# Channel attention over 96 heads: TensorE's instructions rolled into a loop of sixteen heads, hand-made semaphores, single V buffers and 1 MB stores

## The chip, the cores and the metric

The kernel runs on one core of a Trainium2 chip. A core has TensorE (matrix products, PE in the profile), VectorE (DVE), ScalarE (ACT), GpSimd (POOL) and SyncE (SP), each with its own instruction stream, and 16 DMA engines that move data between HBM and the on-chip memory SBUF. TensorE writes into PSUM, a small accumulator memory. The metric is the device time of one execution in microseconds (us), the median over several runs.

## The reference

```python
batch, heads, seq, dim = 8, 12, 512, 64          # Q, K, V: float32
Q_norm = Q / (np.linalg.norm(Q, axis=-2, keepdims=True) + 1e-10)
K_norm = K / (np.linalg.norm(K, axis=-2, keepdims=True) + 1e-10)
attn = np.einsum('bhnd,bhne->bhde', Q_norm, K_norm)
attn = np.exp(attn - np.max(attn, axis=-1, keepdims=True))
attn = attn / (np.sum(attn, axis=-1, keepdims=True) + 1e-10)
return np.einsum('bhnd,bhde->bhne', V, attn).astype(np.float32)
```

For each of 96 heads a 64 x 64 attention matrix between the columns of Q and K is made (each column normed over the 512 rows), a softmax is taken along its rows, and V is multiplied by it. Q, K, V and the output are 12.58 MB each, 50.33 MB in all.

## The kernel before

**Tiling.** Four heads make a unit u (24 of them), two units a pair s (12), two pairs a window w of sixteen heads (6). A row of 128 partitions holds four heads of 32 partitions with 16 sequence rows each.

**The pieces**, named as in the plan of lines 413 to 485, each with the engine that runs it:

- lq, lk, lv (loads, SyncE; lines 178 to 200) and st (stores, SyncE; lines 202 to 210). K of pair 0 is issued from ScalarE's queue (187). One load, K of unit 3, is held back behind a small VectorE write into its buffer (185), and all loads after it too. The store of pair 9, second half, is split (204 to 208): its first half-rows go out as 92, 8 and 28 partitions.
- cq (cast of Q and K to bf16 into qkb, line 216; VectorE, ScalarE or GpSimd), mk (K masked in two copies, 222; VectorE), q2 (squares of Q, 228; ScalarE).
- gr (32 Gram matmuls a unit, 245) and nq (8 matmuls a unit for the norms of Q, 253) on TensorE, into the PSUM tile gram.
- sq, kq, hq, rd, pw, sc (lines 260 to 295): squares, a copy of the cross product, the norms' halves, their sums, the power -1/2 by Ln and Exp, and the scaling of K's side, on VectorE, ScalarE and GpSimd.
- lg (two transposes into logits, 300), ex (four exponentials with their sums, 307; ScalarE), nm (normalised blocks into ab, 316; VectorE).
- cv (cast of V into vb, 234), vt (8 transposes of V on TensorE into vps, 327), vc (their copy into vt, 333), ou (16 output matmuls, four groups a pair, 343) and oc (their copy into so, 351).

**Order.** The class Order (22 to 108) is a list scheduler that runs while the program is built: each piece has costs per engine, pieces it comes after, and a rank; of the pieces that can begin about now the one of the lowest rank is emitted. Its method pause (48) adds waiting time of TensorE for its instruction blocks. Every engine's program, TensorE's included, is then one straight list. The framework puts in the waits between engines. The helper copy (170) records most copies and casts, so in the profile lines 172, 174 and 176 are ScalarE, VectorE and GpSimd copies of many tiles.

**Buffers** (143): three of each of qk32 (2 MB), v32 (1 MB), six so (1 MB), two each of vb, vt, qkb, km, q2, four ab. In PSUM gram has two, vps one, the logits one and po two buffers; the last V transposes use a pool that takes gram's place.

## Time and profile before

| what | value |
|---|---|
| median of 3 runs (lowest to highest) | 127.64 us (127.63 to 127.68) |
| the profiled execution, span | 125.9 us |
| instructions in it | 4630 |
| HBM read and written in it | 37.75 MB and 12.58 MB, 400 GB/s over the span |
| VectorE, ScalarE, TensorE busy | 78%, 72%, 63% |

The span is that of the profiled execution from its first to its last instruction; the timed runs hold some 1.7 us around it. The page of the profile gives, in order: busy time of each engine, the span in 40 equal slices of 3.15 us with digits for tenths, the DMA queues, the chain of work that ended last, the costliest groups of instructions, and the DMA issues. A queue named "instruction" carries the engines' program text; queues of kind "hardware_dynamic" carry data.

### The profile page before, as it was taken

How to read it: one execution, taken by the hardware profiler on the slowest of the kernel's cores; microseconds unless marked ns; L12 is line 12 of the kernel's file. 1: busy time of each engine (PE TensorE's matmuls, PEld its weight loads, DVE VectorE, ACT ScalarE, POOL GpSimd, SP SyncE). 2: the span in 40 equal slices, each digit the busy share in tenths (PEclk: the TensorE clock that was granted, in tenths of full speed). 3: DMA queues.
4: the chain of work that ended last, by engine and by line, in shares of the span. 5: the costliest groups of instructions: out<-in, count | busy, mean ns of one | idle time of the engine just before them, and what ended most of it. 6: DMA issues, size and time to landing. Idle time of an engine off the chain costs nothing.

```text
span 125.9 us, 4630 instructions
## 1 busy us (share of the span) xinstructions
PE 79.6 (63%) x1944; PEld 63.9 (51%) x1944; DVE 98.8 (78%) x198; ACT 91.0 (72%) x217; POOL 50.0 (40%) x68
## 2 busy tenths in 40 slices
PE   0036949258789857766776668676794875976000
PEld 0035848236668745555665555555683764754000
DVE  3189676967959399987999989999979999999200
ACT  4243476579979999499999999999499997670000
POOL 6243353384561836633437226138743551000000
PEclk9999999955555899999999999999779999599555
DMA  3999999999999999999999999999999999999993
GB/s 105 401 419 419 422 414 418 432 424 410 439 409 418 414 433 414 410 431 419 411 428 428 403 419 423 424 424 407 426 413 420 410 415 407 417 411 404 400 411 134
DMA packets 12159, 50.63 MB, mean 402 GB/s; under 512 B 1130, under 2 KB 1130, under 8 KB 10730
## 3 DMA queue, kind: packets, MB, share of 16 engines
q1 hardware_dynamic: 11850, 49.29, 95.9%
q10 hardware_dynamic: 288, 1.05, 2.1%
q8 instruction: 15, 0.25, 0.7%
q14 instruction: 6, 0.05, 0.1%
HBM read 37.75 MB, written 12.58 MB: 400 GB/s over the span
## 4 chain that ended last, share of the span: by engine, by line
DVE 32%; ACT 24%; DMA 18%; PE 8%; issue 7%; POOL 3%; ACTq 0%; SPq 0%; POOLq 0%
DMA out_dram<-so 12%; DVE so L174 12%; DVE km L222 10%; DMA qk<-in_K_dram 6%; PE gram L245 6%; ACT vt L172 5%; ACT q L228 5%; ACT qkb L172 4%; ACT ex L307 4%; DVE ab L316 4%; DVE qkb L174 3%; ACT vb L172 2%; ACT kq L172 2%; POOL vb L176 2%; DVE n L280 1%
## 5 line engine op out<-in xcount | busy, mean ns | idle before, releaser
L245 PE MATMUL gram<-qkb,km 64*128 64x128 bf16 x768 | 33.3, 252 | 23.3 <-DVE km L222 23.3
L245 PEld LDWEIGHTS <-km 64*128 64x128 bf16 x768 | 28.3, 113 | 26.7 <-DVE km L222 26.3
L176 POOL TENSOR_SCALAR qkb<-qk 128x1024 bf16<-128x1024 f32 x24 | 25.4, 1062 | 28.6 <-PE gram L245 19.9
L222 DVE TENSOR_SCALAR km<-qkb,pick 128x1024 bf16<-128x1024 bf16 x48 | 30.3, 671 | 3.0 <-ACT qkb L172 2.4
L174 DVE COPY so<-po 128x512 f32<-128x512 f32 x48 | 30.8, 684 | 0.4
L228 ACT ACTIVATE q<-qk 128x1024 bf16<-128x1024 f32 x24 | 25.5, 1065 | 6.3 <-DMA qk<-in_Q_dram 4.3
L343 PE MATMUL po<-ab,vt 128*32 128x128 bf16 x768 | 20.1, 231 | 9.5 <-DVE so L174 6.9
L172 ACT COPY vt<-vps 128x1024 bf16<-128x1024 bf16 (+1 forms) x26 | 24.5, 956 | 1.2 <-PE vps L327 1.0
L343 PEld LDWEIGHTS <-vt 128*32 128x32 bf16 x768 | 13.4, 100 | 14.9 <-issue 10.7
L327 PE MATMUL vps<-identb,vb 128*128 128x128 bf16 x192 | 16.7, 237 | 3.0 <-ACT vt L172 2.2
L176 POOL TENSOR_SCALAR vb<-v 128x1024 bf16<-128x1024 f32 x13 | 15.0, 1156 | 8.4 <-DMA v<-in_V_dram 8.2
L307 ACT ACTIVATE ex<-lg,r 128x64 f32<-128x64 f32 x48 | 14.5, 325 | 1.6 <-PE lg L300 1.6
L327 PEld LDWEIGHTS <-vb 128*128 128x128 bf16 x192 | 12.6, 106 | 6.0 <-issue 3.1
L174 DVE CAST qkb<-qk 128x1024 bf16<-128x1024 f32 x13 | 12.1, 933 | 4.2 <-DMA qk<-in_K_dram 4.1
L293 POOL TENSOR_TENSOR kqs<-kq,r 128x256 f32<-128x256 f32 x12 | 7.9, 660 | 18.8 <-ACT r L289 8.3
L316 DVE TENSOR_TENSOR ab<-ex,rinv 64x256 bf16<-64x256 f32 x24 | 12.1, 504 | 0.6
L260 DVE SCALAR_TENSOR_TENSOR scr<-gram,eye 128x256 f32<-128x256 f32 x12 | 5.1, 424 | 8.5 <-ACT kq L172 5.7
L172 ACT CAST vb<-v 128x1024 bf16<-128x1024 f32 x11 | 11.7, 1062 | 0.0
L172 ACT CAST qkb<-qk 128x1024 bf16<-128x1024 f32 x11 | 11.6, 1054 | 0.0
L307 ACT ACTIVATION_READ_ACCUMULATOR ex<-lg,r 128x1 f32 x48 | 10.4, 217 | 0.0
L172 ACT COPY kq<-gram 128x256 f32<-128x256 f32 x12 | 4.6, 380 | 7.1 <-PE gram L253 3.1
L253 PEld LDWEIGHTS <-q 128*128 128x128 bf16 x192 | 7.5, 100 | 3.7 <-issue 2.7
(25 smaller groups left out, 41.1 us busy)
## 6 DMA issues: line engine op xcount, KB each, us to landing
out_dram<-so SPq DMA_DIRECT2D x23, 512.0 KB, 9.8
v<-in_V_dram SPq DMA_DIRECT2D x11, 1024.0 KB, 15.8
qk<-in_Q_dram SPq DMA_DIRECT2D x8, 1024.0 KB, 15.9
qk<-in_K_dram SPq DMA_DIRECT2D x8, 1024.0 KB, 17.6
qk<-in_Q_dram SPq DMA_DIRECT2D x8, 512.0 KB, 8.7
qk<-in_K_dram SPq DMA_DIRECT2D x6, 512.0 KB, 9.6
qk<-in_K_dram ACTq DMA_DIRECT2D x2, 512.0 KB
v<-in_V_dram SPq DMA_DIRECT2D x2, 512.0 KB
```

The costliest lines, as they stand in the source:

```text
L172: nc.scalar.copy(o, i)
L174: nc.vector.tensor_copy(o, i)
L176: nc.gpsimd.tensor_scalar(out=o, in0=i, scalar1=1.0, scalar2=0.0, op0=ALU.mult, op1=ALU.add)
L222: nc.vector.tensor_scalar(out=km[u][:, :, a], in0=qkb[u][:, :, 0], scalar1=pick[:, a:a + 1], scalar2=None, op0=ALU.mult)
L228: nc.scalar.activation(q2[u], qk32[s][:, 0, r], AF.Square)
L245: nc.tensor.matmul(gram[s][:, 2 * g + r, 0:2 * D], km[u][rows, t].rearrange("p a d -> p (a d)"), qkb[u][rows, t].rearrange("p x d -> p (x ...
L253: nc.tensor.matmul(gram[s][:, 0, 2 * D + HU * r:2 * D + HU * (r + 1)], q2[u][:, 2 * t:2 * t + 2].rearrange("p t d -> p (t d)"), heads, sta ...
L293: (nc.vector if eng == "DVE" else nc.gpsimd).tensor_tensor(out=kqs[s], in0=kq[s], in1=r8[s][:, 0:HU, None].to_broadcast([128, 4, D]), op=A ...
L307: nc.scalar.activation(e[:, h, :], lg[s][:, h, :], AF.Exp, scale=r8[s][:, HU + h:HU + h + 1], accum_out=z[:, h:h + 1])
L316: nc.vector.tensor_tensor(out=a[half, :, half], in0=e[half], in1=ri[half, :, None].to_broadcast([D, HU, D]), op=ALU.mult,)
L327: nc.tensor.transpose(ps[:, c, n, :], vb[w][:, J * c + j].rearrange("p r d -> p (r d)"), identb)
L343: nc.tensor.matmul(po[s, x][32 * h:32 * (h + 1), j].rearrange("p r d -> p (r d)"), v, ab[s][:, h, :])
```

## The change

The framework's tiles and waits are given up. All buffers are allocated by name, all semaphores by hand, and every piece is a generator of instructions.

- **TensorE.** Its order is written down: FRONT, five turns of one body, BACK. A turn w holds, for the pair n = 2w+2 (EVEN) and n = 2w+3 (ODD), the Gram and norm matmuls, the logits of pair n-1, transposes of V and output groups of the pairs 2w and 2w+1. The body is emitted once, in a hardware loop on TensorE alone. Inside it TensorE takes tokens: it waits until a token semaphore has reached a value and takes that value off again, so that the same instruction serves in every turn.
- **The other engines** keep straight programs, ordered by Order; pause and its parameters are gone, and all ranks and biases are new. A piece that TensorE takes inside the loop counts up a token; every other piece counts up its engine's own counter. Another engine that needs a piece counted by a token waits for a later counted piece of the same engine or for the TensorE piece that took the token.
- **Buffers.** vb and vt have one buffer instead of two, ab two instead of four, v32 four instead of three, so seven instead of six. V is cast by halves of the sequence groups that one half of vt needs.
- **Order of dependencies.** kq comes after sq, hq after kq; sq waits for the norms' matmuls too. lg waits for nm of the pair before.
- **DMA.** A pair is stored as one transfer of 1 MB, except the last, which goes in two of 512 KB. The split store and the held load are gone. SyncE waits before each transfer for the eighth last.

```diff
-    CHUNK, FETCH, FIRST = 256, 6.1, 190
-    def pause(self, begin, cost, n, done):
...
-    NB = dict(qk=3, v=3, vb=2, qkb=2, vt=2, so=6, sm=2, ab=4, km=2, q2=2)
+NQ, NV, NSO = 3, 4, 7
+EVEN = "g0 lg o0 o1 n0 va g1 n1 o2 vb o3".split()
+ODD = "g0 n0 g1 n1 o0 o1 va o2 lg o3 vb".split()
+FRONT = [("nq", 1), ("nq", 0), ("gr", 0), ("gr", 1), ("nq", 2), ("gr", 3), ("lg", 0), ("nq", 3), ("gr", 2), ("vt", 0, 0), ("vt", 0, 1)]
+BACK = [("vt", 5, 3), ("vt", 5, 2), ("ou", 10, 0), ("lg", 11), ("ou", 10, 1), ("ou", 10, 2), ("ou", 10, 3), ("ou", 11, 1), ("ou", 11, 0), ("ou", 11, 3), ("ou", 11, 2)]
...
+    for w in range(W - 1):
+        body = []
+        for half, names in enumerate((EVEN, ODD)):
+            n = 2 * w + 2 + half
+            for it in names:
+                if it[0] == "g":
+                    body.append(("gr", 2 * n + int(it[1])))
+                elif it[0] == "n":
+                    body.append(("nq", 2 * n + int(it[1])))
+                elif it == "lg":
+                    body.append(("lg", n - 1))
+                elif it[0] == "v":
+                    body.append(("vt", w + half, (2 - 2 * half) + (it == "vb")))
+                else:
+                    j = int(it[1])
+                    body.append(("ou", 2 * w + j // 2, 2 * (j % 2) + half))
+        turns.append(body)
...
-        piece(("kq", s), {"ACT": 0.35, "DVE": (0.36, BIAS["kq"])}, [("gr", 2 * s), ("gr", 2 * s + 1), back("sc", s, SM)], [], R["kq"] + 0.01 * s, cross, s)
+        piece(("kq", s), {"ACT": 0.35, "DVE": (0.36, BIAS["kq"])}, [("sq", s), back("sc", s, 2)], [], R["kq"] + G["kq"] * s)
+        piece(("hq", s), {"ACT": 0.1}, [("kq", s), back("rd", s, 2)], [], R["hq"] + G["hq"] * s)
...
-        if HELD == ("l" + "qk"[x], s, r):
-            nc.vector.memset(qk32[s][0:1, x, r, 0, 0:1], 0.0)
...
-        if (s, r) == FEW:
-            for a, b in ((0, 92), (92, 100), (100, 128)):
-                nc.sync.dma_start(out=o[a:b, :J * D], in_=i[a:b, :J * D])
-            nc.sync.dma_start(out=o[:, J * D:], in_=i[:, J * D:])
-            return
+def stored(s):
+    return (0, 1) if s >= S - STS else (None,)
+
+    def store(eng, s, r):
+        o, i = Of[s // 2, s % 2], so[s % NSO].rearrange("p r t d -> p r (t d)")
+        if r is not None:
+            o, i = o[:, r], i[:, r]
+        yield eng.dma_start(out=o, in_=i)
...
+    vb = sbuf("vb", [128, 2 * T, 2, D], BF16)
+    vt = sbuf("vt", [128, J, 128, 4], BF16)
+    ab = sbuf("ab", [128, HU, 2 * D], BF16, 2)
...
+            if k in tokens:
+                last.then_inc(token[token_of(k)], 1)
+            else:
+                last.then_inc(count[e], 1)
+                own[e] += 1
...
+    for k in lane["DMA"]:
+        if k not in early:
+            wait_for("DMA", nc.sync, list(after[k]) + sent[-Order.QUEUE:1 - Order.QUEUE], k)
+            for i in emit[k[0]](nc.sync, *k[1:]):
+                i.then_inc(dma_at[k][0], 16)
+            sent.append(k)
...
+    def tensor_piece(k, looped):
+        need = {}
+        for a in taken.get(k, ()):
+            if a in tokens:
+                need[token_of(a)] = need.get(token_of(a), 0) + 1
+            else:
+                d = engine[a]
+                need[d] = max(need.get(d, 0), value[a])
+        for n, v in need.items():
+            if n in token:
+                nc.tensor.wait_ge(token[n], v).then_inc(token[n], -v)
+            else:
+                nc.tensor.wait_ge(count[n], v)
+        for i in emit[k[0]]("PE", *k[1:]):
+            pass
+        i.then_inc(count["PE"], 1)
...
+    for k in front:
+        tensor_piece(k, False)
...
+    with nc.tensor.Fori(0, len(turns)):
+        for k in full:
+            tensor_piece(k, True)
+    for k in behind:
+        tensor_piece(k, False)
```

## The prediction

> **What bounds the kernel now.** I read the DMA rows of the page first, then its queue table, then the busy time by stage, then what SyncE's queue and TensorE wait for.

> ```profile
> PE 79.6 (63%) x1944; PEld 63.9 (51%) x1944; DVE 98.8 (78%) x198; ACT 91.0 (72%) x217; POOL 50.0 (40%) x68
> ...
> DMA  3999999999999999999999999999999999999993
> GB/s 105 401 419 419 422 414 418 432 424 410 439 409 418 414 433 414 410 431 419 411 428 428 403 419 423 424 424 407 426 413 420 410 415 407 417 411 404 400 411 134
> ...
> q1 hardware_dynamic: 11850, 49.29, 95.9%
> ...
> q8 instruction: 15, 0.25, 0.7%
> ```

> No engine is above 78%, but the 16 DMA engines are full in every slice except the first and the last. 50.33 MB of Q, K, V and output have to pass, and they pass at 400 to 439 GB/s from end to end. The queue table says what else is in that stream: 15 instruction fetches of 16 KB. They are TensorE's, since 3888 of its instructions over 15 fetches are one per 259, and 0.25 MB over 3888 is 64 bytes each. Their price: 0.7% of 16 engines over 125.9 us is 14.1 us of engine time, 0.94 us each.

> ```profile
> 12.60:112.00 99.40, 73.26 (x1764) 59.01 (x1759) 86.00 (x178) 86.09 (x213) 44.88 (x46) 0.88 1.02 419
> 112.00:119.00 7.00, 3.26 (x128) 2.06 (x127) 5.37 (x9) 0.51 (x2) 0.00 (x0) 0.85 1.02 399
> 119.00:123.00 4.00, 0.00 (x0) 0.00 (x0) 0.00 (x0) 0.00 (x0) 0.00 (x0) 0.50 0.99 404
> 123.00:126.00 3.00, 0.00 (x0) 0.00 (x0) 0.00 (x0) 0.00 (x0) 0.00 (x0) 0.50 0.29 119
> ```

> The columns are the busy time of PE, PEld, DVE, ACT and POOL, the granted clock, the DMA share and GB/s. Over the middle 99.4 us VectorE is idle 13.4 us (2.8 us in each 20.6 us that two pairs of units take, a turn of the new loop), and computing ends at 117.4 us, while the DMA engines stay full to about 123 us. So the end is set by bytes; computing is some us ahead.

> ```profile
> SPq L189 <- DVE qkb L174: 10.0, 6, 4.0
> SPq L198 <- ACT vb L172: 9.9, 3, 5.3
> ...
> SPq L210 <- DMA out_dram<-so: 8.0, 11, 1.0
> ```

> ```profile
> v<-in_V_dram SPq DMA_DIRECT2D x11, 1024.0 KB, 15.8
> ```

> ```profile
> PE gram L245 <- DVE km L222: 23.3, 18, 8.3
> PE po L343 <- DVE so L174: 6.9, 19, 1.0
> ```

> The first fence is SyncE's waits (us in total, times, longest), the second the page's DMA issues (size, median us to landing), the third TensorE's waits. SyncE does wait for buffers that computing frees, but what it issues lands 15.8 us later, of which the transfer itself is 2.5 us (1.05 MB at 419 GB/s). Some 13 us of queued transfers lie ahead of it: that is the cover of every edit to the compute side. TensorE waits most for the masked K, and for nothing that looks like a missing instruction.

> **The change, part by part.** The profiled execution's span is 125.9 us, the median of the runs 127.64, so 1.7 us lie around the span; I keep them.

> *The TensorE loop.* One turn holds 4 Gram groups of 32 matmuls, 4 norm groups of 8, 2 logit pairs, 4 V transposes of 8 and 8 output groups of 16: 324 matmuls. Five turns are 1620; the straight front has 178, the back 146, together 1944 as now, so the work is the same. The text shrinks from 3888 to 2 x (178 + 324 + 146) = 1296 instructions and some 60 waits. At 256 to a fetch these are 5 fetches instead of 15. If the body (648 instructions and about 26 token waits, 2.6 blocks) stays in the instruction memory over its turns, 10 fetches go: 10 x 0.94 / 16 = 0.59 us off the DMA stream. If it doesn't stay, nothing goes, and each of the 4 taken branches back stalls TensorE. No backward branch is in this trace, so that stall is bounded: below by 0, above by two fetches in a row, each about 1.2 us from block boundary to the packet's start (the trace's packet times against TensorE's 256th, 512th, ... instruction) and 0.94 us of packet, 4.3 us. I take 0, since before shows fetches keeping up with TensorE, and hold the other end for a rival.

> *Tokens and own semaphores.* About 26 waits a turn on TensorE's sequencer; the one such instruction before TensorE's work in this trace takes 0.05 us, 1.3 us a turn, beside 20.6 - 14 = 6 us in which TensorE is idle: 0. On the other engines, an extra semaphore instruction between two operations leaves the gap between them as small as without one (the trace's 22 cases on VectorE, median gap below zero, as the next one overlaps): 0. Operations counted by a token are seen by others only through a later operation or through TensorE, so a V buffer or a finished output row is released later by one or two operations, 1 to 2 us. Behind that wait on SyncE's queue stand all later loads and stores; the 13 us above cover it. Without that cover it would cost the delay itself, 1 to 2 us at a place.

> *Single V buffers (vb, vt), two instead of four ab, four v32, seven so.* A V copy now waits until the outputs that read the same half of vt are done. In the order EVEN, ODD the outputs of half k=0 all stand in EVEN, the transposes into that half in ODD, and the other way round, so each has half a turn (10 us) against a copy of 1 us (ACT vt, 956 ns). Cost 0 behind that; if a copy came late, the 16 matmuls of an output group (0.43 us) and their store come late with it.

> *Serial order kq after sq, hq after kq.* The chain from Gram to logits gets longer by at most 0.42 + 0.38 us (scr 424 ns, kq 380 ns). Between n1 and the logits that need them stand at least five other TensorE pieces; 0 behind these.

> *Stores of 1 MB and the fewer-partition store.* Both kernels store a pair when all four copies are done, so nothing waits longer for a larger store. Transfers issued: 72 before (23 + 11 + 8 + 8 + 8 + 6 + 2 + 2 and the 4 of L207/L208), 58 after (32 of Q and K, 13 V, 13 stores). In the trace's packet records a DMA's 16 semaphore packets take 9 ns each: 14 x 16 x 9 / 16 engines = 0.13 us. The split of L206 goes: 256 packets of 2 KB at 91 ns become 128 of 4 KB at 161 ns, (23.3 - 20.6) / 16 = 0.17 us. [...]

> *Start.* The held load (L185, SyncE's queue idle 2.7 to 7.3 us) goes; the second slice shows 401 instead of 419 GB/s, worth at most 3.15 x 18 / 419 = 0.14 us. The constants now wait for each other on GpSimd, done well before the first data at 5.5 us. I take 0 for both.

> Sum on the DMA stream: 0.59 + 0.17 + 0.13 = 0.89 us of packet time. Packet records overlap a little (share 1.02 to 1.03), so 0.85 us of span: 125.0 us, and 126.8 us as the runs count. The end is ragged now (rate falls from 122.5 to 124.7 us; about 0.9 us is lost there), and it can fall out 0.5 us either way: 126.2 to 127.4 for this case.

> **Rivals.**

> A (slower): the branch back misses. For it: the fetches of before follow TensorE block by block, one per crossing and to the very end, as of a memory that holds little more than the next block; the body is 2.6 blocks. Against it: nothing in this trace runs code twice. The price is up to 4.3 us of TensorE at each of four turns, beside 2.8 us a turn that VectorE has to spare; 1.5 us a turn stay, 6 us over four. Computing may end about 3 us later than 117.4 before the last stores (two of 1.2 us and their landing) run past 124.7, and from there it decides. With no fetch saved: 127.64 + 3 = 130.6 at the upper bound; with 2.1 us a miss, within the spare time, nothing is lost. I put it at 129.5. [...]

> B: the branch doesn't stall, or its stall is hidden, but every turn fetches its blocks anew. 13 to 15 fetches again, 0.30 us left of the gain: 127.35, at the edge of what a measurement tells.

> C (slower as well): the fixed TensorE order and the later releases starve the DMA engines in some stage. For it: SyncE waits 10.0 us for qkb and 9.9 us for vb already. Against: the queue is 13 us deep and VectorE's and ScalarE's work is the same. Half a us a turn over five turns is 2.5 us: 127.64 - 0.85 + 2.5 = 129.3.

> **How the numbers follow.** My forecast case has 0.47, A 0.19, B 0.12, C 0.22. About 0.2% (0.26 us) is what a measurement of this kernel can tell from no change, so faster means below 127.38. The forecast case lies there except for 0.04, B with half: 0.43 + 0.06 = 0.49. Same: 0.04 + 0.05 from these, and 0.02 from A with a short miss: 0.11. Slower: the rest of A and C and 0.01 of B, 0.40. The time is that of the likeliest case, 126.8. The range runs from 126.1 (all gains and a tidier end) to 130.6 (A at its upper bound); about 0.05 lies below it, 0.12 above.

> **What would show it.** TensorE's instruction queue with about 5 packets instead of 15, at the front, in the first turn and at the end: the loop stays; with 13 or more: B or A. Gaps of 2 us or more on TensorE at the start of each turn, ended by nothing the profile shows: A. DMA share of 9 in every slice from 2 to 38, near 419 GB/s: the forecast; a slice below 9 with SyncE waiting for so, vb or qkb: C. Last compute after 120 us: A or C. I am wrong if the time is above 127.4, and wrong in the reason if it is faster with 15 fetches.

## The result, and the profile after

The change makes the kernel slower.

| kernel | median (lowest to highest) | ratio to before, 95% interval | profiled span | last copy out ends | last data packet ends |
|---|---|---|---|---|---|
| before | 127.66 us (127.63 to 127.78) | 1 | 125.9 us | 117.4 us | 124.7 us |
| after | 134.59 us (133.76 to 134.85) | 1.052 [1.049, 1.055] | 133.0 us | 126.9 us | 131.2 us |

The page of the changed kernel, the rows that answer to those of before:

```profile
PE 80.8 (61%) x1944; PEld 65.8 (49%) x1944; DVE 98.0 (74%) x202; ACT 97.4 (73%) x221; POOL 36.5 (27%) x54
...
DMA  3999999999999999999999999999999999249492
GB/s 103 407 420 428 414 403 418 410 430 398 424 410 411 403 411 413 415 418 421 419 415 419 416 410 421 415 416 421 419 409 410 419 416 414 106 170 400 191 403 110
...
q1 hardware_dynamic: 11520, 49.29, 91.5%
...
q8 instruction: 5, 0.08, 0.3%
```

Five instruction fetches in place of 15, and none of them between 43.1 and 118.6 us, while the four branches back stand at 47.6, 65.0, 84.8 and 99.5: the later turns bring no fetch. But the DMA engines run dry in slices 35, 36 and 38 (113 to 126 us): all loads are done and the stores wait for results. The same stages of both kernels, after first; the columns are the busy time of PE, PEld, DVE, ACT, POOL, the granted clock, the DMA share and GB/s:

```profile
50.00:80.00 30.00, 23.55 (x608) 18.83 (x608) 27.33 (x56) 26.67 (x60) 10.99 (x11) 0.83 1.02 416
80.00:107.00 27.00, 16.39 (x390) 13.30 (x394) 22.39 (x47) 21.50 (x54) 7.13 (x8) 0.80 1.02 417
107.00:119.00 12.00, 11.16 (x294) 9.20 (x282) 11.31 (x27) 11.33 (x31) 1.97 (x4) 0.88 0.66 264
119.00:128.00 9.00, 3.90 (x130) 2.82 (x130) 7.77 (x13) 3.37 (x11) 0.37 (x1) 0.76 0.82 321
```

```profile
50.00:80.00 30.00, 21.36 (x619) 17.06 (x617) 27.57 (x57) 28.27 (x69) 13.56 (x14) 1.00 1.02 419
80.00:107.00 27.00, 18.89 (x507) 15.43 (x509) 25.19 (x52) 23.76 (x58) 12.85 (x13) 0.93 1.02 417
107.00:119.00 12.00, 8.03 (x232) 5.56 (x222) 10.18 (x20) 4.30 (x13) 0.00 (x0) 0.78 1.02 406
```

Up to 107 us the DMA share is the same 1.02, so the DMA row tells nothing of what goes wrong; the computing columns do. Before, VectorE works 25.2 of 27 us between 80 and 107 us; after, 22.4, and what is left undone stands behind 107 us. TensorE's waits in the changed kernel (us in total, times, longest):

```profile
PE gram L356 <- ACT q L336: 9.7, 1, 9.7
PE vps L410 <- PEq L658: 8.0, 3, 4.9
PE po L422 <- PEq L658: 6.8, 7, 3.1
PE gram L349 <- PEq L658: 5.4, 4, 4.0
PE vps L410 <- DVE vb L302: 5.4, 1, 5.4
```

The first row is the start, when no data is ready yet. PEq L658 is TensorE's sequencer at a token. Before, two thirds of its waiting (23.3 of 36.2 us) was for masked K; now each kind of piece in its fixed order waits for something in turn. In the timeline (start, length) one such wait and the end of VectorE's work read:

```profile
103.96 1.89 PE L349 MATMUL gram<-qkb,km 64*128 64x128 bf16 x32 [3.99 <-PEq L658]
...
125.65 1.28 DVE L302 COPY so<-po 128x512 f32<-128x512 f32 x2
```

The end of VectorE's work in the kernel before, nine copies in a row to 117.4 us:

```profile
111.88 5.48 DVE L174 COPY so<-po 128x512 f32<-128x512 f32 x9
```

The Gram group above, at a granted clock of 0.5, takes 1.89 us; a group at full clock takes 1.07 in the trace of before. How far the two have come, from the starts of the Gram groups and the ends of the copies out:

| us | Gram u4 | u8 | u12 | u16 | u20 | u23 | last copy of pair 0 | pair 6 | pair 11 |
|---|---|---|---|---|---|---|---|---|---|
| before | 20.3 | 38.8 | 54.3 | 71.2 | 88.9 | 99.7 | 50.8 | 92.8 | 117.4 |
| after | 29.2 | 48.7 | 65.8 | 85.6 | 104.0 | 113.2 | 39.2 | 95.7 | 126.9 |

Before runs its Gram matrices far ahead and does outputs late and fast; after does outputs early and Gram matrices late.

### The profile page after: what moved, and what is told of

Read it like the earlier page. It is cut to its first block, busy times and chain, and to the rows that moved or that the text cites. A ratio compares the mean times of both kernels' runs of the same rounds, so it can differ in the third digit from the quotient of the medians.

```text
span 133.0 us, 4711 instructions
## 1 busy us (share of the span) xinstructions
PE 80.8 (61%) x1944; PEld 65.8 (49%) x1944; DVE 98.0 (74%) x202; ACT 97.4 (73%) x221; POOL 36.5 (27%) x54
## 3 DMA queue, kind: packets, MB, share of 16 engines
q1 hardware_dynamic: 11520, 49.29, 91.5%
q10 hardware_dynamic: 288, 1.05, 2.1%
## 5 line engine op out<-in xcount | busy, mean ns | idle before, releaser
L349 PEld LDWEIGHTS gram<-qkb,km 64*128 64x128 bf16 x768 | 29.5, 115 | 11.6 <-issue 8.5
L300 ACT CAST qkb<-qk 128x1024 bf16<-128x1024 f32 x24 | 25.1, 1048 | 3.1 <-PE gram L349 3.1
L300 ACT COPY vt<-vps 128x1024 bf16<-128x1024 bf16 x20 | 20.3, 1016 | 5.9 <-PE vps L410 5.9
L410 PEld LDWEIGHTS vps<-identb,vb 128*128 128x128 bf16 x176 | 12.6, 113 | 17.0 <-issue 9.1
L422 PEld LDWEIGHTS po<-ab,vt 128*32 128x32 bf16 x736 | 12.7, 107 | 14.0 <-issue 11.0
L404 DVE TENSOR_TENSOR ab<-ex,ri 64x256 bf16<-64x256 f32 x24 | 14.2, 591 | 0.6
L356 PE MATMUL gram<-heads,q 128*128 128x4 bf16 x192 | 8.5, 167 | 9.7 <-ACT q L336 9.7
L302 DVE CAST vb<-v 128x1024 bf16<-128x1024 f32 x18 | 13.3, 754 | 0.2
L356 PEld LDWEIGHTS gram<-heads,q 128*128 128x128 bf16 x192 | 6.7, 99 | 12.4 <-issue 10.6
L391 PE MATMUL lg<-ident,kqs 128*128 128x128 f32 x24 | 6.9, 381 | 1.9 <-PEq L658 1.1
## 6 DMA issues: line engine op xcount, KB each, us to landing
v<-in_V_dram SPq DMA_DIRECT2D x11, 1024.0 KB, 18.6
out_dram<-so SPq DMA_DIRECT2D x11, 1024.0 KB, 12.6
qk<-in_Q_dram SPq DMA_DIRECT2D x8, 1024.0 KB, 15.3
qk<-in_K_dram SPq DMA_DIRECT2D x8, 1024.0 KB, 17.4
```

Source lines behind the costliest of these rows:

```text
L300: return nc.scalar.copy(o, i)
L302: return nc.vector.tensor_copy(o, i)
L349: yield nc.tensor.matmul(gram[s % 2][:, 2 * g + r, 0:2 * D], km[u % 2][rows, t].rearrange("p a d -> p (a d)"), qkb[u % 2][rows, t].rearran ...
L356: yield nc.tensor.matmul(gram[s % 2][:, 0, 2 * D + HU * r:2 * D + HU * (r + 1)], q2[u % 2][:, 2 * t:2 * t + 2].rearrange("p t d -> p (t d) ...
L404: yield nc.vector.tensor_tensor(out=ab[s % 2][half, :, half], in0=ex[s % 2][half], in1=ri[s % 2][half, :, None].to_broadcast([D, HU, D]), ...
L410: yield nc.tensor.transpose(v_bank(w, q)[:, c, n, :], vb[:, J * c + 2 * q + n].rearrange("p r d -> p (r d)"), identb)
```

## The experiments

Eighteen kernels, each timed beside the kernel before (127.68 to 127.86 us).

**1. Are the loop, the tokens or the buffers to blame?** First TensorE's loop is written out straight, tokens kept:

```diff
-    with nc.tensor.Fori(0, len(turns)):
-        for k in full:
+    for t in turns:
+        for k in t:
             tensor_piece(k, True)
```

> The changed kernel with its TensorE loop written out straight: five turns one after the other, same tokens, same order everywhere. Theory O (the fixed order of TensorE leaves no slack, so every late piece adds to the end): 134.6 us as the changed kernel, within 0.6, with 15 instruction fetches instead of 5. Theory L (the loop itself costs: the branch back of 0.2 us, the first pass over its blocks, the token handling at the branch): 1.5 us or more faster, 133 or below.

Measured 143.88 us (140.94 to 144.38), what neither theory said; the fastest of its runs is still 6.35 us above the changed kernel. Fifteen fetches are back. TensorE's groups in this trace (busy, mean ns, idle before and what ended it):

```profile
L349 PE MATMUL gram<-qkb,km 64*128 64x128 bf16 x768 | 36.5, 265 | 9.9 <-issue 3.9 <-PEq L658 3.3 <-DVE km L332 2.5
L422 PE MATMUL po<-ab,vt 128*32 128x128 bf16 x736 | 21.4, 252 | 10.9 <-issue 6.6 <-PEq L658 2.1 <-DVE ab L404 1.4
```

"issue", 10.5 us in these two rows, is waiting that no semaphore explains. It falls into seven gaps of 0.87 to 2.13 us, at the 1217th, 1473rd, 1985th, 2241st, 2497th, 2753rd and 3009th instruction: multiples of 256 apart, and 256 is what one fetch brings in the trace of before (16 KB at 64 bytes an instruction). I take them for blocks of text that come late. In the loop there is one such gap (1.26 us, first turn). So tokens in straight text cost more than tokens in the loop; why they bring so many late blocks was not tried. Next the tokens go too, and plain counters take their place:

```diff
-    in_loop = {k for t in turns for k in t}
+    in_loop = set()
```

> As the straight one, and no tokens: every piece counts up its engine's own counter, so that every engine sees a finished piece at once, and TensorE waits on counters. Theory O: within 0.6 us of the straight one. Theory T (pieces counted by tokens are seen late, as the store of pair 7 that is issued 6.8 us after its last copy, and buffers come free late): 2 us or more faster than the straight one.

Measured 134.58 us (133.33 to 134.94), ratio 1.052 [1.047, 1.057], last copy at 127.4 us, three late blocks (3.4 us). By its letter this is theory T's sign, but what comes back is what e1 had lost beyond the loop. Against the changed kernel nothing is gained: the loop, the tokens and the later view of their pieces do not, taken together, cost the 7 us. What each is worth alone is open, since e2 has 2.1 us more of late blocks than the loop. On this base two vb, two vt and four ab, waits loosened to match, TensorE's order kept:

```diff
-    vb = sbuf("vb", [128, 2 * T, 2, D], BF16)
-    vt = sbuf("vt", [128, J, 128, 4], BF16)
-    ab = sbuf("ab", [128, HU, 2 * D], BF16, 2)
+    vb = sbuf("vb", [128, 2 * T, 2, D], BF16, 2)
+    vt = sbuf("vt", [128, J, 128, 4], BF16, 2)
+    ab = sbuf("ab", [128, HU, 2 * D], BF16, 4)
```

> As the one without tokens, with two vb, two vt and four ab as before, and their waits relaxed accordingly; the order of every engine is kept. Theory O: within 0.7 us of the one without tokens, since the long waits of TensorE in the changed kernel are for V casts, the copy out of the single vps bank, the masked K and a po bank, none of which these buffers hold. Theory B (the single V buffers and the two ab couple the stages): 3 us or more faster.

138.72 us (138.10 to 139.16): slower still. With three v32 and six so to make room, the V transposes wait for casts of V:

```profile
PE vps L410 <- DVE vb L302: 20.8, 4, 6.6
```

The orders of the other engines were not kept, though. With the loosened waits the planner drew new ones: VectorE has 205 operations in place of 202, and its casts of V, masks and copies out follow each other differently. So this run prices neither the buffers nor the order by itself; theory B stays untested.

**2. The order.** The base of e2 takes every engine's order and assignment from the kernel before, with its buffers (two vb, two vt, four ab, three v32, six so), 512 KB stores and its dependencies of sq, kq, hq and rd:

```diff
+ORDER = [(("lq", 0, 0), "DMA"), ...]
-    front, turns, back_ = tensor_order()
+    front, turns, back_ = [k for k, e in ORDER if e == "PE"], [], []
```

> The changed kernel's machinery (buffers by name, hand-made counters, no framework waits, everything straight) running the order of before on every engine, with the buffer counts of before and stores of 512 KB. Theory O: 127.6 us as before, within 0.8, DMA full to the end, last compute near 117.4 us. Theory W (the hand-made waits, which stand as instructions of their own, cost time on the engines): 130 us or more, with last compute after 120 us.

130.43 us (130.33 to 130.52), ratio 1.021 [1.020, 1.023]; last copy at 121.5 us: what theory W had said. Whether the hand-made waits are the reason is taken up under 6. Order, assignment, these dependencies and the buffers that they need are worth 134.58 - 130.43 = 4.15 us, measured together.

**3. What does a delay cost?** TensorE is made late, in the changed order and in the kernel before:

```diff
-        for t in range(T):
+        for t in list(range(T)) * (4 if u == 10 else 1):
```

> The changed kernel written straight with counted semaphores (134.6 us by itself), and TensorE made late on purpose: the 32 matmuls of gr(10) are issued four times over, 96 matmuls more, the last pass of which leaves the same sums. One pass takes 1.1 us at the full clock and 1.9 us at half, so TensorE is held 3.3 to 5.7 us longer at that place. Theory O (the new order couples TensorE so closely to the other engines that a delay anywhere is handed on to the end): the time grows by most of the delay, 137 to 140 us. Theory L (the loss is made at a few places, above all at the end, and the DMA engines cover a delay in the middle): 134.6 within 0.7 us.

> The kernel before with the same 96 matmuls more in gr(10). Theory O says that its order has slack there, since its Gram matrices run far ahead of its outputs: 127.7 to 128.5 us, a quarter of the delay at most. The rival, that TensorE's lateness costs the same in both kernels: 130 to 133 us.

136.48 us (135.50 to 136.77), 1.9 more than e2 and between its two theories; and 130.09 us (129.78 to 130.56), 2.4 more than before, as the rival said. Theory O falls: before has no more slack than after. In the trace of e9 Gram u11 starts 3.7 us later, and the last copy ends at 121.3, 3.9 later. Its stages:

```profile
80.00:107.00 27.00, 19.61 (x537) 16.09 (x536) 23.96 (x50) 24.42 (x57) 14.06 (x15) 0.94 1.02 417
107.00:119.00 12.00, 8.15 (x244) 5.96 (x243) 11.58 (x24) 6.99 (x25) 0.61 (x1) 0.95 0.91 359
```

The DMA engines are full to 107 us here too, and computing made up nothing: work that is late at 50 us is as late at 117. Of the 3.9 us the transfers hid 1.5. (In e8 the last copy is only 0.6 us later than in e2, 128.0 against 127.4, and the last data packet 2.1; what lengthens that tail was not followed up.) The same with VectorE, whose masks of unit 10 are made four times over:

```diff
-        for a in range(2):
+        for a in list(range(2)) * (4 if u == 10 else 1):
```

> The kernel before with the two masks of unit 10 computed four times over, six VectorE instructions of 0.44 us more, 2.6 us in all. If VectorE's program is as close to the end as TensorE's proved to be (3.7 us late there cost 2.4): 129 to 129.8 us. If VectorE has slack that TensorE has not: 127.5 to 128.2 us.

129.17 us (128.41 to 129.79), 1.5 more than before for 2.6 us of work; last copy at 121.1.

**4. Parts of the order.** Turn 0 stands straight in front of the loop, with gr of units 4 and 5 ahead of the first V transposes (the planner draws the other engines' orders anew):

```diff
-FRONT = [("nq", 1), ("nq", 0), ("gr", 0), ("gr", 1), ("nq", 2), ("gr", 3), ("lg", 0), ("nq", 3), ("gr", 2), ("vt", 0, 0), ("vt", 0, 1)]
+FRONT = [..., ("lg", 0), ("gr", 4), ("nq", 4), ("lg", 1), ("gr", 5), ("nq", 5), ("vt", 0, 0), ("vt", 0, 1), ...]
```

> The changed kernel with its loop, but the first turn stands straight in front of it with the Gram matrices of units 4 and 5 ahead of the first V transposes, so that TensorE no longer waits 5.4 us for the cast of V at 20.7 us; the loop runs four turns. Theory O (each delay is handed on to the end): 3 us and more come back, 129 to 131.5 us. The rival, that the end is set by what happens late and the wait at the front is absorbed: 133.5 to 135.2 us.

134.28 us (133.50 to 135.47), not to be told from the changed kernel. Gram u4 starts at 24.0 in place of 29.2, but u6 at 40.4 in place of 36.9, and the last copy at 126.3: the wait was moved, not removed. Next, twelve casts of V from VectorE to GpSimd:

```diff
+    order = [(k, "POOL" if k[0] == "cv" and e == "DVE" and (k[2] == 1 or k[1] in (1, 3)) else e) for k, e in order]
```

> The changed kernel with twelve of VectorE's eighteen casts of V given to GpSimd (the kernel before gave it thirteen); the order on every engine stays otherwise. GpSimd is idle two thirds of the span, and VectorE loses 12 x 0.75 = 9.0 us of its 98.0. If the amount of VectorE's work sets the end: 127 to 131 us. Rival (the path runs through the fixed orders of all engines, and VectorE's sum is not on it): 133.5 to 135.5 us.

133.87 us (132.14 to 135.46), last copy 126.8, as the rival said: VectorE's sum does not set the end. Then the planner's costs are replaced by measured ones, and, in a second kernel, assignment, ranks and the order inside the turn as well:

```diff
+COST = {("gr", "PE"): 1.35, ("vt", "PE"): 0.8, ("nm", "DVE"): 1.3, ("mk", "DVE"): 0.95, ...}
```

> The changed kernel with its loop, tokens, buffers and TensorE's order; only the planner's costs are replaced by the durations that the trace of the changed kernel shows (a Gram group 1.35 us in the mean in place of 1.2, eight V transposes 0.8 for 0.65, normalising 1.3 for 1.05, a pair of masks 0.95 for 0.8, and so on), with no exclusion of VectorE and GpSimd. Theory P (the plan was drawn with durations that the chip does not keep, and the orders that came of it wait for each other): the last copy comes 3 us earlier, 130.5 to 132.5 us. Rival (the loss belongs to TensorE's order, to the tokens or to the single buffers): 133.5 us or more.

> The changed kernel's loop, tokens, single buffers and 1 MB stores, with another assignment and order throughout, planned with the measured durations: all casts of V on GpSimd, all casts of K on VectorE, all copies out on ScalarE, and the order within TensorE's turn changed. Theory P: the structure costs nothing by itself and another order takes back most of the loss, 127.5 to 130.5 us. Rival (the structure of a fixed turn with single buffers costs the 7 us whatever the order): 133 us or more.

133.10 us (132.68 to 133.45), last copy 125.5; and 134.20 us (132.83 to 137.23), last copy 124.3 in the profiled execution. The first lies between the theories, the second with the rival: measured costs give back 1.5 of the 7 us, and of the orders tried for a fixed turn of sixteen heads none came near the kernel before.

**5. The stores.** The kernel before with 1 MB stores (its planner drew new orders for them):

```diff
-        for r in range(2):
+        for r in ((None,) if s < S - 1 else range(2)):
```

> The kernel before with nothing changed but its stores: one transfer of 1 MB for each pair in place of two of 512 KB, the last pair in two halves, and no store in four parts. If the size of the stores neither helps nor hurts while the queues are full (my prediction's price, -0.17 us with the four parts gone): 127.3 to 128.0 us. If the coarser stores start later and leave the DMA engines idle at the end: over 128.5 us.

130.90 us (130.27 to 131.09), last copy at 122.8 in place of 117.4: the new plan computes later. It says little of the store's size by itself, and much of how easily a plan is lost. In the changed kernel 4 MB of stores go ahead of the last load of K (1.5 MB before), which lands at 103.0 us in place of 94.3. Is computing late for want of that load? The trace of the changed kernel answers by itself. A cast for the last unit starts 7 us after that load has landed, and what it waited for is a Gram group, which frees the bf16 buffer:

```profile
110.44 1.04 POOL L303 TENSOR_SCALAR qkb<-qk 128x1024 bf16<-128x1024 f32 x1 [3.39 <-PE gram L349]
```

In the kernel before the last of these casts starts 2.3 us after the landing, at 96.6. A run that issues the stores behind the load:

```diff
+    early = [k for k in dma[:dma.index(("lk", S - 1, 1))] if k[0] == "st"]
+    dma = [k for k in dma if k not in early]
+    n = dma.index(("lk", S - 1, 1)) + 1
+    lanes["DMA"] = dma[:n] + early + dma[n:]
```

> The changed kernel with its loop, tokens and the order of every engine, except that SyncE issues the four stores that stood ahead of the last load of K right behind it; seven output buffers are enough for that. Theory T (the early stores take the DMA engines' time from Q and K, and the late pairs are computed late for want of data): the last K lands up to 10 us earlier and the last copy comes 3 us earlier or more, 129 to 132 us. Theory C (the loads are issued late because the computation frees their buffers late; transfers ahead of them cost nothing): the last copy stays within 1.5 us of 126.9, the DMA engines idle in the middle instead of the end, 133 to 137 us.

140.62 us (138.52 to 142.91). The last K lands 6 us earlier, at 96.9, and the last copy ends 7 us later, at 133.9. VectorE's waits:

```profile
DVE so L302 <- PE po L422: 10.4, 5, 4.7
...
DVE so L302 <- DMA out_dram<-so: 5.3, 1, 5.3
```

Now a copy waits for the store that empties its buffer, so this run alone would not decide; with the row above it, theory T falls. That the loads are late because computing frees their buffers late, as theory C has it, fits and is not shown. The time is above what theory C said, too: seven so were not enough.

**6. The rest: one dependency, and addresses.** In e7's trace TensorE waits for something that the kernel before does not have:

```profile
PE lg L476 <- DVE ab L489: 5.1, 4, 1.7
```

The logits wait for the pair before to be normalised. Put back, on e7 and on e2:

```diff
-        piece(("lg", s), {"PE": 0.4}, [("sc", s), back("nm", s, 1)], [before["lg", s]], 0)
+        piece(("lg", s), {"PE": 0.4}, [("sc", s), back("ex", s, 1)], [before["lg", s]], 0)
```

> The kernel before's order on the changed kernel's machinery (130.4 us by itself) with one dependency put back as the kernel before has it: the logits of a pair wait for the exponentials of the pair before and not for its normalising. In that run's trace TensorE waited 5.1 us in four places for VectorE's normalising ahead of the logits. If this dependency holds the rest of the loss: 128 to 129 us. If the rest is elsewhere (instruction blocks that come late, the last transposes not halved): 129.8 to 130.6 us.

> The changed kernel written straight with counters (134.6 us) and the same one dependency loosened: logits after the exponentials of the pair before. TensorE waits only 1.9 us ahead of logits in the changed kernel, and its order has the logits late: 133.8 to 134.8 us. Under 133 us would say that this dependency is a good part of the 7 us.

On e7 130.15 us (130.09 to 130.23): the last copy comes 3.0 us earlier, at 118.5, and the time falls by 0.3 only. On e2 134.32 us (133.54 to 135.49), nothing. So in e14 something other than computing holds the end: the transfers. The DMA view from 20 to 50 us, where only loads pass, of before and of e14:

```profile
DMA packets 2644, 12.65 MB, mean 422 GB/s; under 512 B 192, under 2 KB 192, under 8 KB 2014
```

```profile
DMA packets 2621, 12.40 MB, mean 413 GB/s; under 512 B 190, under 2 KB 190, under 8 KB 2032
```

Engines full in both (DMA share 1.02), 2% fewer bytes. The first buffer of e14, as of the changed kernel, begins at 16,512 B in each partition, and all that transfers touch begin 128 B behind a multiple of 512. Those of the kernel before begin on one: two unused constants (front, pad) stand ahead of them, which the change drops. Three kernels move nothing but addresses (the first on e14, the second the changed kernel itself, the third the kernel before, displaced):

```diff
+    sbuf("front", [128, 96], F32)
     qk32 = sbuf("qk", [128, 2, 2, T, D], F32, NQ)
```

```diff
-    const.tile([128, D // 4], F32, name="front")
+    const.tile([128, D // 4 + 32], F32, name="front")
```

> The run before (order and dependencies of the kernel before on the changed kernel's machinery, 130.15 us) with 384 unused bytes a partition ahead of the first buffer, so that every buffer that a transfer touches begins on a multiple of 512 B. If the address makes the packets longer: a packet of 4 KB takes 160 ns again, 4.20 MB move in 10 us, and the time falls by 1.5 to 2.5 us, 127.6 to 128.7 us. If the packets are longer for another reason: 163 to 164 ns and 130.1 us within 0.3.

> The changed kernel itself with the same 384 bytes ahead of its first buffer and nothing else changed. Packets of 4 KB in 160 ns. Its end waits for the computation (last copy at 126.9 us, DMA engines starving from 107 us), so that faster transfers are worth less than in the run above: 133 to 134.6 us if the computation is not held by the loads, 132 to 133 us if it follows them.

> The kernel before with its unused first tile 128 B longer, so that every buffer begins 128 B behind a multiple of 512 B, as in the changed kernel; its plan and all its instructions stay. If the address is the cause: packets of 4 KB in 163 to 164 ns, 4.11 MB in 10 us, and 129.2 to 130.3 us. If not: 127.7 us within 0.3.

The same view of e17 and of the displaced kernel before:

```profile
DMA packets 2653, 12.64 MB, mean 421 GB/s; under 512 B 198, under 2 KB 198, under 8 KB 2028
```

```profile
DMA packets 2605, 12.40 MB, mean 413 GB/s; under 512 B 190, under 2 KB 190, under 8 KB 2000
```

| kernel | start behind 512 B | 4 KB packet, 20 to 50 us | 8 KB packet | time | last copy | last data packet |
|---|---|---|---|---|---|---|
| before | 0 | 159.7 ns | 310.6 ns | 127.69 us | 117.4 | 124.7 |
| e19, before displaced | 128 | 163.6 ns | 315.5 ns | 129.10 us (129.06 to 129.32) | 119.1 | 126.2 |
| e14 | 128 | 163.8 ns | 314.7 ns | 130.15 us (130.09 to 130.23) | 118.5 | 126.8 |
| e17, e14 in place | 0 | 159.9 ns | 309.8 ns | 128.50 us (128.38 to 128.75) | 117.2 | 125.1 |
| after | 128 | 163.4 ns | 316.3 ns | 134.59 us (133.76 to 134.85) | 126.9 | 131.2 |
| e18, after in place | 0 | 159.9 ns | 309.9 ns | 133.65 us (133.25 to 136.50) | 126.0 | 130.2 |

The address is the cause: 1.4 us lost in the kernel before, 1.65 regained in e17, ratio there 1.006 [1.004, 1.008]. In the changed kernel, whose end waits for computing, 0.9, which is within the spread of its runs. Theory W, that hand-made waits cost e7 its 2.7 us, is left with the 0.8 us that remain.

## Why the prediction was wrong

The 6.9 us come apart along one line of kernels, from after to before: loop and tokens 0.0 (134.59 to e2's 134.58), order with its assignment and buffers 4.15 (to e7's 130.43), the logits' dependency 0.3 (to e14's 130.15), addresses 1.65 (to e17's 128.50), and 0.8 left (to 127.69). Of these 0.8 the last data packet is 0.3 us late, and from it to the last instruction pass 1.67 us in place of 1.16; what makes these differ was not tried. The split depends on the order of the steps. With the addresses put right first (e18) they are worth 0.9, and order, dependencies and buffers together 5.15 (133.65 to e17's 128.50): with displaced buffers the last data packet of e7 ends at 126.9 us and that of e14 at 126.8, though the last copy of e14 comes 3.0 us earlier.

- *The loop stays, 15 fetches become 5*: right. The branch back takes 0.21 to 0.23 us on TensorE's sequencer, and its matmuls run on across each of the four. With no fetch after 43.1 us, ahead of the first branch, until 118.6, rivals A and B are out. That a branch back costs two fetches in a row, 4.3 us, as A's price has it, was an assumption; no run shows it.
- *0.89 us less packet time*: right in kind. All packets together take 124.57 us per DMA engine before and 123.31 in e18, 1.26 less. But displaced, as the change has them, they take 125.15. That the packets themselves keep their length was assumed by saying nothing of the two dropped constants; this is the term the sum lacked.
- *"The 13 us above cover it", "Cost 0 behind that"* (single buffers, later releases, the serial order): this is the step that failed, with the fixed order of TensorE, which the sum put at nothing outside rival C. Thirteen us of queued transfers keep the DMA engines busy, but do not give computing its time back. VectorE and ScalarE work 27.6 and 28.3 of the 30 us from 50 to 80 in the kernel before; a delay there is not made up (in e9 3.7 us late at Gram u11, 3.9 at the last copy), and what counts is the lead at the end.
- *That lead, "about 3 us"*: too large. In the runs whose computing decides, the last packet ends 5.4 to 5.9 us after the last copy (e7, e9, e13; with the changed kernel's stores 4.3). Before ends its packets at 124.7, so computing decides once the last copy passes some 119 us, 1.5 us after its 117.4. The changed order is 9.5 us late.
- *Rival C* came nearest, with a chance of 0.22 and a price of 2.5 us in place of 7: I took half a us a turn. The DMA engines do starve, though only at the end. Of its two causes the later releases through tokens cost nothing on balance (e2); that the other, TensorE's fixed order, does it alone is not shown, since e7 changes all engines' orders and the buffers at once. The table of Gram starts shows how it goes instead: 8.9 us are lost before u4, ahead of which the written-down order has V transposes (and their loads and casts), 13.5 by u23, and the drain behind u23 (13.7 us against 17.7) gives some back. That the front moved in e4 without moving the end says that the loss does not sit at one place.
- *What stays open*: which part of the order costs how much. The front, VectorE's sum and the planner's costs, changed one at a time, gave 0.3, 0.7 and 1.5 us, the first two within the spread of the runs; holding stores back made it worse. Only the whole order of the kernel before gave 4.15, and that with its buffers, whose own share is not known (e3 changed orders too). Whether a periodic turn exists that does as well was not settled. None of the eighteen beats the kernel before.

## What to carry to other kernels

Full DMA engines do not show that computing has time to spare (in e9 their share was 1.02 from 80 to 107 us, and 3.7 us of delay still cost 2.4): put a few us of delay on one engine and see whether the end moves. When buffers are allocated by hand, give those that transfers touch the alignment they had: 128 B of displacement cost the kernel before 1.4 us, 1% of its time (e19). An order that was tuned as a whole can't be judged by its parts' dependencies; keep it fixed while the machinery under it is changed, and only then change it.
